# Modulation stage of a hybrid diffusion layer: plain fp32 products, a scale row and one shift addition

## The chip, the cores and the metric

The kernel runs as one program on one core of a Trainium2 chip. The metric is device time in microseconds (us) from launch to end. The kernel before took 2781.36 us (median of three runs, 2778.57 to 2790.45). Its profiled execution took 2780.29 us, of which the trace covers a span of 2778.5 us.

## The reference

One layer works on 2048 latent tokens and 256 context tokens of width 1024. What matters here is its first step:

```
c_act = silu(c);  cctx_act = silu(c_ctx)
mod_lat = c_act @ ada_w + ada_b          # 6 parts of 1024: sh1, sc1, g1, sh2, sc2, g2
mod_ctx = cctx_act @ ada_w + ada_b
h_ctx = rmsnorm(ctx, norm1_g) * (1 + csc1) + csh1
h_lat = rmsnorm(x + pos, norm1_g) * (1 + sc1) + sh1
proj = h @ w_in                          # for both streams, then three token mixers
x = x + g1 * (y @ w_out);  x = x + g2 * sq_relu_mlp(...);  out = rmsnorm(x, final_g)
```

The norm divides each token by its root mean square. The factor (1 + sc1) * norm1_g and the shift sh1 belong to the 1024 features and are the same for all latent tokens; the context has its own pair.

## The kernel before, in words

The engines are TensorE (PE; its weight loads are PEld), VectorE (DVE), ScalarE (ACT), GpSimd (POOL) and SyncE (SP), which issues nearly all DMAs. PE runs its instructions in the order in which the program writes them. The orders of the other engines come from a scheduler that goes by priorities; `high_priority` raises them. Each engine works through its own list in order, so an instruction that waits holds up all behind it.

The first stage has these steps, with the lines of the kernel before:

- Modulation (L265 to L298). The first 2048 columns of `ada_w` (shift and scale) come in 32 tiles `aw` of 128x512. Each is split for the product into a rounded part (ACT, L274) and a rest (DVE or POOL, L275), both of the type fp32r, and two products (L276, L277) add into four PSUM tiles `m`. The rows are copied (L285), transposed (L287) and added to the bias, so that `mT` (shift) and `sc1` (scale) hold one feature per partition and a column for each stream.
- Norm (`norm_in`, L240, with `rstd_of`, L212). A tile is 128 tokens, one per partition, 1024 features along it. There are 18: t0 and t1 are context, t2 to t17 latents. For a latent tile POOL adds two position parts (L237, L238). ACT squares and sums (L251) and takes a first reciprocal root (L215, L216), DVE corrects it in three small operations (L218, L221, L225) and multiplies the tile by both factors (L253).
- Modulate (`modulate`, L436). PE transposes a tile in two halves of four blocks (L444), so that features lie on partitions. DVE (L448, five blocks) and ACT (L450, three blocks) read them from PSUM with the block's scale and shift into `hy`; ACT rounds (L451) into `hTh`, and DVE or POOL takes the rest (L452) into `hTl`. In the loop the norm of tile i+2 is written ahead of the modulate of tile i; the first four tiles are normed before the loop.
- Products. Five token groups: group 0 is t0 and t1, the others four latent tiles each. Two weight blocks are loaded and split beforehand (L312, L313), and the products of a group with them (L365 to L367, three per feature block) are slipped in behind the tiles of the next group by a `Filler`. The last group's products follow the loop, and after them come the other projections and the mixers.

The token tiles `xt` have four buffers: t4's load has to wait for the transposes of t0, and so on.

Of the kernel before, what the change touches and what calls it, by code (L numbers as in the profile page):

```python
# [20 lines left out]
P = 128  # L21
# [90 lines left out]
def body(ctx: ExitStack, tc: tile.TileContext, I, out, dbg=None, stage=99):  # L112
# [16 lines left out]
    def trt():  # L129
        return ps.tile([P, 512], F32, name="tr", bufs=1)  # L130
# [44 lines left out]
    csp = const.tile([P, KC, 4], F32R, name="csp")  # L175
# [7 lines left out]
    nc.vector.tensor_copy(csp[:, :, 0:2], cact)  # L183
    nc.vector.tensor_tensor(csp[:, :, 2:4], cact, csp[:, :, 0:2].bitcast(F32), op=ALU.subtract)
# [55 lines left out]
    def norm_in(g, j):  # L240
        t0 = GRP[g][0]
        xt = nrm.tile([P, D], F32, name="xt", bufs=4)
        if g == 0:
            nc.sync.dma_start(xt, cx[j * P:(j + 1) * P, :])
        else:
            i = (t0 - CTX) // P + j
            nc.sync.dma_start(xt, x[i * P:(i + 1) * P, :])
            add_pos(nrm, posc, i, xt)
        ss = nrm.tile([P, 1], F32, name="ss", bufs=3)
        junk = nrm.tile([P, D], mybir.dt.bfloat16, name="junk", bufs=1)  # L250
        nc.scalar.activation(junk, xt, AF.Square, accum_out=ss)  # L251
        r0, r1 = rstd_of(nrm, ss, 1, D, "n1")
        nc.vector.tensor_scalar(xt, xt, r0, r1, op0=ALU.mult, op1=ALU.mult)  # L253
        return xt
# [11 lines left out]
    for k in range(KC):  # L266
        for j in range(4):
            i = 4 * k + j
            with tc.high_priority(PRI + 1500):
                aw = adp.tile([P, 512], F32, name="aw", bufs=8)  # L270
                nc.sync.dma_start(aw, ada_w[k * P:(k + 1) * P, 512 * j:512 * j + 512])
                ah = adp.tile([P, 512], F32R, name="awh", bufs=3)
                al = adp.tile([P, 512], F32R, name="awl", bufs=3)
                nc.scalar.copy(ah, aw)  # L274
                (nc.gpsimd if i % 5 in (0, 2) else nc.vector).tensor_tensor(al, aw, ah.bitcast(F32), op=ALU.subtract)  # L275
            nc.tensor.matmul(mps[j][0:4, :], csp[:, k, :], ah, start=k == 0, stop=False)  # L276
            nc.tensor.matmul(mps[j][0:2, :], csp[:, k, 0:2], al, start=False, stop=k == KC - 1)  # L277
# [3 lines left out]

    mtp = trt()
    for j in range(4):
        mrow = adp.tile([4, 512], F32, name="mrow", bufs=2)
        (nc.vector.tensor_copy if j % 2 else nc.scalar.copy)(mrow, mps[j][0:4, :])  # L285
        for i in range(4):
            nc.tensor.transpose(mtp[:, 16 * j + 4 * i:16 * j + 4 * i + 4], mrow[:, i * P:(i + 1) * P], ident[0:4, 0:4])  # L287
# [3 lines left out]
    mtv = mtp[:, 0:64].rearrange("p (j s) -> p j s", s=4)  # L291
    nc.vector.tensor_tensor(mT, mtv[:, :, 0:2],
                            pcol("ab", 0, 16).unsqueeze(2).to_broadcast([P, 16, 2]), op=ALU.add)
    nc.vector.tensor_tensor(mT, mT, mtv[:, :, 2:4], op=ALU.add)
# [141 lines left out]
    def modulate(g, j, xt):  # L436
        s = 1 if g == 0 else 0
        ts_ = slice(j * P, (j + 1) * P)
        for hf in range(2):
# [5 lines left out]
            for k in range(4):  # L445
                kk = 4 * hf + k
                if k < 2 + hf:
                    nc.vector.tensor_scalar(y[:, k, :], tp[:, k, :], sc1[:, kk, s:s + 1], mT[:, kk, s:s + 1], op0=ALU.mult, op1=ALU.add)  # L448
                else:
                    nc.scalar.activation(y[:, k, :], tp[:, k, :], AF.Identity, scale=sc1[:, kk, s:s + 1], bias=mT[:, kk, s:s + 1])  # L450
# [3 lines left out]
    for i, (g, j) in enumerate(tiles):  # L454
        if NA <= i + 2 < len(tiles):
            xts[tiles[i + 2]] = norm_in(*tiles[i + 2])
        modulate(g, j, xts.pop((g, j)))
# [1361 lines left out]
```

## Time and profile before

| | before |
|---|---|
| median of three runs | 2781.36 us |
| profiled execution | 2780.29 us |
| span of its trace | 2778.5 us |
| first stage, up to the last group's first product | 138.4 us |
| PE busy over the span | 92% |

The profile names a group of instructions by line, engine, operation and tiles. Busy time is the time in which an engine had an instruction running; idle time before an instruction is put down to what released it. The granted clock is a share of TensorE's full rate.

### The profile page before, as it was taken

How to read it: one execution, taken by the hardware profiler on the slowest of the kernel's cores; microseconds unless marked ns; L12 is line 12 of the kernel's file. 1: busy time of each engine (PE TensorE's matmuls, PEld its weight loads, DVE VectorE, ACT ScalarE, POOL GpSimd, SP SyncE). 2: the span in 40 equal slices, each digit the busy share in tenths (PEclk: the TensorE clock that was granted, in tenths of full speed). 3: DMA queues.
4: the chain of work that ended last, by engine and by line, in shares of the span. 5: the costliest groups of instructions: out<-in, count | busy, mean ns of one | idle time of the engine just before them, and what ended most of it. 6: DMA issues, size and time to landing. Idle time of an engine off the chain costs nothing. (4 is left out here: it accounts for less than half of the span.)

```text
span 2778.5 us, 36372 instructions
## 1 busy us (share of the span) xinstructions
PE 2561.5 (92%) x12239; PEld 2081.4 (75%) x12239; DVE 1754.9 (63%) x3039; ACT 1161.4 (42%) x2053; POOL 982.4 (35%) x868
## 2 busy tenths in 40 slices
PE   5798889899999888888897999989999999999997
PEld 3676667788887676777776888867887888888876
DVE  7855476146646986656665787666666356545586
ACT  6755521133335666433334444544445332222343
POOL 5734411245444443334443343343432122222221
PEclk8999989999999999989998999999999999999999
DMA  7443355565656666766663777555554677656564
GB/s 221 143 138 110 95 159 163 155 159 157 156 153 174 183 177 187 242 192 203 233 204 104 205 211 223 171 183 163 144 156 139 221 244 242 211 176 202 169 210 152
DMA packets 490215, 495.24 MB, mean 178 GB/s; under 512 B 88226, under 2 KB 371580, under 8 KB 490028
## 3 DMA queue, kind: packets, MB, share of 16 engines
q1 hardware_dynamic: 464076, 465.58, 55.7%
q10 hardware_dynamic: 20480, 15.73, 1.7%
q0 software_dynamic: 5472, 11.60, 1.5%
q8 instruction: 97, 1.59, 0.2%
q14 instruction: 90, 0.74, 0.1%
HBM read 336.89 MB, written 155.92 MB: 177 GB/s over the span
## 5 line engine op out<-in xcount | busy, mean ns | idle before, releaser
L365 PE MATMUL pp<-hTh,whi 128*128 128x512 f32 (+1 forms) x1048 | 435.6, 416 | 14.5 <-DVE evt L505 10.9
L367 PE MATMUL pp<-hTh,wlo 128*128 128x512 f32 (+1 forms) x1048 | 410.4, 392 | 1.7 <-POOL wlo L313 1.3
L366 PE MATMUL pp<-hTl,whi 128*128 128x512 f32 (+1 forms) x1048 | 408.8, 390 | 0.2 <-DVE hTl L452 0.2
L1780 PE MATMUL yps<-bh,al 128*128 128x512 f32 x832 | 326.5, 392 | 3.8 <-POOL al L1405 2.4
L1778 PE MATMUL yps<-bh,ah 128*128 128x512 f32 x832 | 325.7, 392 | 0.0
L1779 PE MATMUL yps<-bl,ah 128*128 128x512 f32 x832 | 324.2, 390 | 0.0
L1405 POOL TENSOR_TENSOR al<-ar,ah 128x1024 fp32r<-128x1024 f32 x54 | 132.6, 2455 | 481.3 <-ACT ah L1642 470.8
L365 PEld LDWEIGHTS pp<-hTh,whi 128*128 128x128 f32 x1048 | 206.0, 197 | 52.0 <-DVE evt L505 12.7
L1642 ACT CAST ah<-ar 128x1024 fp32r<-128x1024 f32 x108 | 113.5, 1051 | 306.2 <-PE yps L1779 270.4
L367 PEld LDWEIGHTS pp<-hTh,wlo 128*128 128x128 f32 x1048 | 204.7, 195 | 45.6 <-POOL wlo L313 3.5
L366 PEld LDWEIGHTS pp<-hTl,whi 128*128 128x128 f32 x1048 | 205.6, 196 | 35.5 <-issue 1.9
L1780 PEld LDWEIGHTS yps<-bh,al 128*128 128x128 f32 x832 | 156.2, 188 | 42.9 <-POOL al L1405 4.3
L1779 PEld LDWEIGHTS yps<-bl,ah 128*128 128x128 f32 x832 | 156.3, 188 | 33.4
L1778 PEld LDWEIGHTS yps<-bh,ah 128*128 128x128 f32 x832 | 156.4, 188 | 31.9
L1408 POOL TENSOR_TENSOR uz<-tz 128x512 f32<-128x512 f32 x32 | 49.8, 1556 | 345.2 <-ACT whi L1413 176.2
L1478 PE MATMUL accy<-th,whi 128*128 128x512 f32 x384 | 152.6, 397 | 2.2 <-ACT th L1642 1.2
L1480 PE MATMUL accy<-th,wlo 128*128 128x512 f32 x384 | 150.7, 392 | 2.6 <-DVE wlo L1405 2.6
L1479 PE MATMUL accy<-tl,whi 128*128 128x512 f32 x384 | 151.0, 393 | 0.0
L1405 DVE TENSOR_TENSOR wlo<-wab,whi 128x512 fp32r<-128x512 f32 x124 | 115.2, 931 | 36.3 <-ACT whi L1413 36.3
L1405 DVE TENSOR_TENSOR wlo<-ws,whi 128x512 fp32r<-128x512 f32 x93 | 78.5, 845 | 81.8 <-ACT whi L1413 81.5
L1413 ACT CAST whi<-wab 128x512 fp32r<-128x512 f32 x124 | 76.7, 619 | 120.3 <-PE accy L1479 54.8
L1264 PE MATMUL pp<-woh,yh 128*128 128x512 f32 x256 | 106.2, 415 | 9.0 <-ACT yh L1250 9.0
(407 smaller groups left out, 6040.1 us busy)
## 6 DMA issues: line engine op xcount, KB each, us to landing
uD<-uz SPq DMA_DIRECT2D x224, 256.0 KB
ar<-uD SPq DMA_DIRECT2D x108, 512.0 KB
braw<-in_mlp_w_dram SPq DMA_DIRECT2D x84, 512.0 KB
wab<-in_mlp_w_dram SPq DMA_DIRECT2D x62, 512.0 KB
maw<-in_ada_w_dram SPq DMA_DIRECT2D x64, 256.0 KB
wraw<-in_w_in_dram SPq DMA_DIRECT2D x54, 256.0 KB
rb<-rD SPq DMA_DIRECT2D x96, 128.0 KB
aw<-in_ada_w_dram SPq DMA_DIRECT2D x32, 256.0 KB
```

The costliest lines, as they stand in the source:

```text
L365: nc.tensor.matmul(acc[:, 0:n], hi, hTh[g][:, k, :], start=k == 0, stop=False)
L366: nc.tensor.matmul(acc[:, 0:n], hi, hTl[g][:, k, :], start=False, stop=False)
L367: nc.tensor.matmul(acc[:, 0:n], lo, hTh[g][:, k, :], start=False, stop=k == KC - 1)
L1264: nc.tensor.matmul(acc, yh[:, k, :], woh[:, k, ns], start=k == 0, stop=False)
L1405: eng.tensor_tensor(o, a, b, op=ALU.subtract)
L1478: nc.tensor.matmul(acc, hi[:, k, :], T2[i][0][:, k, :], start=first and k == 0, stop=False, skip_group_check=True)
L1479: nc.tensor.matmul(acc, hi[:, k, :], T2[i][1][:, k, :], start=False, stop=False, skip_group_check=True)
L1480: nc.tensor.matmul(acc, lo[:, k, :], T2[i][0][:, k, :], start=False, stop=k == 3, skip_group_check=True)
L1642: nc.scalar.copy(hi, r_)
L1778: nc.tensor.matmul(acc, ah[:, p_, :], bh, start=p_ == 0, stop=False)
L1779: nc.tensor.matmul(acc, ah[:, p_, :], bl, start=False, stop=False)
L1780: nc.tensor.matmul(acc, al[:, p_, :], bh, start=False, stop=p_ == 7)
```

## The change

- `ada_w` tiles are no longer split: one plain fp32 product of each tile with `cact` takes the place of two fp32r products, and `csp` goes.
- The latents' scale is also built as a row: the bias and norm gain come in as rows of 1024 (`arow`, `nrow`, two small loads on SP), two additions and two products on one partition give (1 + scale) * gain, and two plain fp32 products with a column of ones spread it over 128 partitions into `scB` (copied from PSUM by ACT and DVE).
- For a latent tile the norm's last multiplication is gone. The two factors are multiplied with each other (128x1), and `modulate` multiplies the tile by that and by `scB` ahead of the transposes (after L450). Out of PSUM comes one addition of the shift per half (after L458, DVE) where five DVE and three ACT operations stood. Context tiles keep the old way.

Line numbers differ between the two kernels; L456 of the kernel after is the transpose of L444, L463 and L465 are L448 and L450, L467 is L452, L322 and L323 are L312 and L313, L215, L218 and L222 the norm's small operations.

DVE's list of the kernel before, from the last context operations to the first latent ones (`tp_575` and `tp_587` are t1's transposes, `tp_618` t2's first half):

```order
L448 TENSOR_SCALAR hy<-tp_575,sc_494,mT 128x128 x2
L448 TENSOR_SCALAR hy<-tp_587,sc_494,mT 128x128 x3
L218 TENSOR_SCALAR n1v<-ss 128x1
L312 CAST whi<-evt 128x512
L452 TENSOR_TENSOR hTl_87<-hy,hTh_86 128x4x128
L313 TENSOR_TENSOR wlo<-evt,whi 128x512
L218 TENSOR_SCALAR n1v<-ss 128x1
L221 SCALAR_TENSOR_TENSOR n1t<-n1r,n1v 128x1
L225 TENSOR_SCALAR n1t<-n1t 128x1
L253 TENSOR_SCALAR xt<-xt,n1r,n1t 128x1024
```

The same stretch of DVE's list in the kernel after (`n1r` and `n1t` from here on are t2's and t3's factors, `row_297` the scale row, `pp` the spread row, `tp_404` t0's transposes):

```order
L215 TENSOR_SCALAR n1v<-ss 128x1 x2
L218 SCALAR_TENSOR_TENSOR n1t<-n1r,n1v 128x1 x2
L222 TENSOR_SCALAR n1t<-n1t 128x1 x2
L253 TENSOR_TENSOR n1r<-n1r,n1t 128x1 x2
L291 SCALAR_TENSOR_TENSOR row_297<-row_297,mrow 1x512 x2
L292 TENSOR_TENSOR row_297<-row_297,row_296 1x512 x2
L322 CAST whi<-wraw 128x512
L323 TENSOR_TENSOR wlo<-wraw,whi 128x512
L322 CAST whi<-wraw 128x512
L298 COPY scB<-pp 128x512
L322 CAST whi<-evt 128x512 x2
L323 TENSOR_TENSOR wlo<-wraw,whi 128x512
```

Before, both context tiles are modulated ahead of the factors of t2 and t3. Now the factors of t2 and t3 stand first, the row behind them, and the context tiles' L463 come only after eight weight operations and the copy L298 more (three of these weight operations lie behind the rows shown).

PE's list of the kernel before, from the last modulation product to t2's transposes (`m` are the PSUM tiles of the modulation, `tp_551` to `tp_587` the context's transposes):

```order
L277 MATMUL m_199<-awl,csp 2x512
L279 MATMUL tr<-ident,pr 128x128
L287 MATMUL tr<-ident,mrow 128x4 x16
L444 MATMUL tp_551<-ident,xt 128x128 x4
L444 MATMUL tp_563<-ident,xt 128x128 x4
L444 MATMUL tp_575<-ident,xt 128x128 x4
L444 MATMUL tp_587<-ident,xt 128x128 x4
L444 MATMUL tp_618<-ident,xt 128x128 x4
```

And the same place in the kernel after:

```order
L271 MATMUL m_196<-aw,cact 2x512
L273 MATMUL tr<-ident,pr 128x128
L294 MATMUL tr<-ident,mrow 128x2 x16
L297 MATMUL pp<-row_297,row_298 128x512 x2
L456 MATMUL tp_404<-ident,xt 128x128 x4
L456 MATMUL tp_416<-ident,xt 128x128 x4
L456 MATMUL tp_428<-ident,xt 128x128 x4
L456 MATMUL tp_440<-ident,xt 128x128 x4
```

The two products that spread the row now stand between the modulation and the context's transposes. From the end of the first stage on, the lists of all engines are the same in both kernels.

```diff
--- before.py
+++ after.py
@@ -172,7 +172,6 @@
     crt = trt()
     nc.tensor.transpose(crt[:, 0:2 * KC], cr, ident[0:2 * KC, 0:2 * KC])
     cact = const.tile([P, KC, 2], F32, name="cact")
-    csp = const.tile([P, KC, 4], F32R, name="csp")
     sgt = const.tile([P, 2 * KC], F32, name="sgt")
     nc.vector.tensor_scalar(sgt, crt[:, 0:2 * KC], -87.0, None, op0=ALU.max)
     nc.scalar.activation(sgt, sgt, AF.Exp, scale=-1.0)
@@ -180,8 +179,6 @@
     nc.vector.reciprocal(sgt, sgt)
     nc.vector.tensor_tensor(cact, crt[:, 0:2 * KC].rearrange("p (s k) -> p k s", s=2),
                             sgt.rearrange("p (s k) -> p k s", s=2), op=ALU.mult)
-    nc.vector.tensor_copy(csp[:, :, 0:2], cact)
-    nc.vector.tensor_tensor(csp[:, :, 2:4], cact, csp[:, :, 0:2].bitcast(F32), op=ALU.subtract)
     pr = sm.tile([P, P], F32, name="pr")
     nc.vector.memset(pr, 0.0)
     srcs = [
@@ -250,8 +247,11 @@
         junk = nrm.tile([P, D], mybir.dt.bfloat16, name="junk", bufs=1)
         nc.scalar.activation(junk, xt, AF.Square, accum_out=ss)
         r0, r1 = rstd_of(nrm, ss, 1, D, "n1")
-        nc.vector.tensor_scalar(xt, xt, r0, r1, op0=ALU.mult, op1=ALU.mult)
-        return xt
+        if g == 0:
+            nc.vector.tensor_scalar(xt, xt, r0, r1, op0=ALU.mult, op1=ALU.mult)
+            return xt, None
+        nc.vector.tensor_tensor(r0, r0, r1, op=ALU.mult)
+        return xt, r0
 
     tiles = [(g, j) for g in range(5) for j in range(GRP[g][1] // P)]
     xts = {}
@@ -265,33 +265,43 @@
     mps = [pm0.tile([P, 512], F32, name=f"m{i}") for i in range(4)]
     for k in range(KC):
         for j in range(4):
-            i = 4 * k + j
             with tc.high_priority(PRI + 1500):
                 aw = adp.tile([P, 512], F32, name="aw", bufs=8)
                 nc.sync.dma_start(aw, ada_w[k * P:(k + 1) * P, 512 * j:512 * j + 512])
-                ah = adp.tile([P, 512], F32R, name="awh", bufs=3)
-                al = adp.tile([P, 512], F32R, name="awl", bufs=3)
-                nc.scalar.copy(ah, aw)
-                (nc.gpsimd if i % 5 in (0, 2) else nc.vector).tensor_tensor(al, aw, ah.bitcast(F32), op=ALU.subtract)
-            nc.tensor.matmul(mps[j][0:4, :], csp[:, k, :], ah, start=k == 0, stop=False)
-            nc.tensor.matmul(mps[j][0:2, :], csp[:, k, 0:2], al, start=False, stop=k == KC - 1)
+            nc.tensor.matmul(mps[j][0:2, :], cact[:, k, :], aw, start=k == 0, stop=k == KC - 1)
     prt = trt()
     nc.tensor.transpose(prt[:, 0:P], pr, ident)
     nc.vector.tensor_copy(prm, prt[:, 0:P])
 
+
+    nrow, arow, ones1 = [adp.tile([1, w_], F32, name=f"row{w_}{i}") for i, w_ in enumerate((D, D, P))]
+    with tc.high_priority(PRI + 1000):
+        nc.sync.dma_start(nrow, I["norm1_g"])
+        nc.sync.dma_start(arow, ada_b[D:2 * D].rearrange("(o n) -> o n", o=1))
+    hot = ExitStack()
+    hot.enter_context(tc.high_priority(PRI + 1500))
+    nc.vector.memset(ones1, 1.0)
     mtp = trt()
-    for j in range(4):
-        mrow = adp.tile([4, 512], F32, name="mrow", bufs=2)
-        (nc.vector.tensor_copy if j % 2 else nc.scalar.copy)(mrow, mps[j][0:4, :])
+    scB = sm.tile([P, D], F32, name="scB")
+    for j in (2, 3, 0, 1):
+        mrow = adp.tile([2, 512], F32, name="mrow", bufs=4)
+        (nc.vector.tensor_copy if j % 2 else nc.scalar.copy)(mrow, mps[j][0:2, :])
+        if j >= 2:
+            js = slice(512 * j - D, 512 * j - D + 512)
+            nc.vector.scalar_tensor_tensor(arow[:, js], arow[:, js], 1.0, mrow[0:1, :], op0=ALU.add, op1=ALU.add)
+            nc.vector.tensor_tensor(arow[:, js], arow[:, js], nrow[:, js], op=ALU.mult)
         for i in range(4):
-            nc.tensor.transpose(mtp[:, 16 * j + 4 * i:16 * j + 4 * i + 4], mrow[:, i * P:(i + 1) * P], ident[0:4, 0:4])
+            nc.tensor.transpose(mtp[:, 8 * j + 2 * i:8 * j + 2 * i + 2], mrow[:, i * P:(i + 1) * P], ident[0:2, 0:2])
+    for hf in range(2):
+        sb = pp()
+        nc.tensor.matmul(sb, ones1, arow[:, 512 * hf:512 * hf + 512])
+        (nc.vector.tensor_copy if hf else nc.scalar.copy)(scB[:, 512 * hf:512 * hf + 512], sb)
+    hot.close()
     adst.close()
     alloc_h(spool(hlat, "hp4", "left"), 4)
     mT = const.tile([P, 16, 2], F32, name="mT")
-    mtv = mtp[:, 0:64].rearrange("p (j s) -> p j s", s=4)
-    nc.vector.tensor_tensor(mT, mtv[:, :, 0:2],
-                            pcol("ab", 0, 16).unsqueeze(2).to_broadcast([P, 16, 2]), op=ALU.add)
-    nc.vector.tensor_tensor(mT, mT, mtv[:, :, 2:4], op=ALU.add)
+    mtv = mtp[:, 0:32].rearrange("p (j s) -> p j s", s=2)
+    nc.vector.tensor_tensor(mT, mtv, pcol("ab", 0, 16).unsqueeze(2).to_broadcast([P, 16, 2]), op=ALU.add)
 
     sc1 = const.tile([P, KC, 2], F32, name="sc1")
     nc.vector.scalar_tensor_tensor(sc1, mT[:, 8:16, :], 1.0, pcol("n1", 0, KC).unsqueeze(2).to_broadcast([P, KC, 2]),
@@ -433,28 +443,33 @@
     wxa = [load_half(w_in, [(C_XA, 0, P)], P, hf, w0 if hf else None, True) for hf in range(2)]
     pt0 = psum(p0, "pt0")
 
-    def modulate(g, j, xt):
+    def modulate(g, j, xt, rs):
         s = 1 if g == 0 else 0
         ts_ = slice(j * P, (j + 1) * P)
+        if g:
+            nc.vector.scalar_tensor_tensor(xt, xt, rs, scB, op0=ALU.mult, op1=ALU.mult)
         for hf in range(2):
             tp = pt0.tile([P, 4, P], F32, name="tp0", bufs=4)
             y = nrm.tile([P, 4, P], F32, name="hy", bufs=3)
             ks = slice(4 * hf, 4 * hf + 4)
             for k in range(4):
                 nc.tensor.transpose(tp[:, k, :], xt[:, (4 * hf + k) * P:(4 * hf + k + 1) * P], ident)
-            for k in range(4):
-                kk = 4 * hf + k
-                if k < 2 + hf:
-                    nc.vector.tensor_scalar(y[:, k, :], tp[:, k, :], sc1[:, kk, s:s + 1], mT[:, kk, s:s + 1], op0=ALU.mult, op1=ALU.add)
-                else:
-                    nc.scalar.activation(y[:, k, :], tp[:, k, :], AF.Identity, scale=sc1[:, kk, s:s + 1], bias=mT[:, kk, s:s + 1])
+            if g:
+                nc.vector.tensor_tensor(y, tp, mT[:, ks, 0:1].to_broadcast([P, 4, P]), op=ALU.add)
+            else:
+                for k in range(4):
+                    kk = 4 * hf + k
+                    if k < 2 + hf:
+                        nc.vector.tensor_scalar(y[:, k, :], tp[:, k, :], sc1[:, kk, s:s + 1], mT[:, kk, s:s + 1], op0=ALU.mult, op1=ALU.add)
+                    else:
+                        nc.scalar.activation(y[:, k, :], tp[:, k, :], AF.Identity, scale=sc1[:, kk, s:s + 1], bias=mT[:, kk, s:s + 1])
             nc.scalar.copy(hTh[g][:, ks, ts_], y)
             (nc.gpsimd if hf else nc.vector).tensor_tensor(hTl[g][:, ks, ts_], y, hTh[g][:, ks, ts_].bitcast(F32), op=ALU.subtract)
 
     for i, (g, j) in enumerate(tiles):
         if NA <= i + 2 < len(tiles):
             xts[tiles[i + 2]] = norm_in(*tiles[i + 2])
-        modulate(g, j, xts.pop((g, j)))
+        modulate(g, j, *xts.pop((g, j)))
         if g and j == 1:
             fil.add(f"first{g - 1}", first(g - 1), GRP[g - 1][1] / 50)
         fil.run(2.7)
```

## Rows read from the trace of the kernel before

**Rows 1.** The page: busy time, share of the span and instructions.
```profile
PE 2561.5 (92%) x12239; PEld 2081.4 (75%) x12239; DVE 1754.9 (63%) x3039; ACT 1161.4 (42%) x2053; POOL 982.4 (35%) x868
```

**Rows 2.** Stretches from:to: length, busy (instructions) per engine, clock, DMA share, GB/s.
```profile
30.00:56.00 26.00, 13.70 (x68) 10.06 (x68) 20.20 (x44) 12.47 (x30) 12.79 (x11) 0.61 0.81 205
56.00:139.00 83.00, 59.57 (x297) 49.37 (x295) 73.56 (x158) 63.93 (x153) 61.55 (x48) 0.88 0.45 136
139.00:165.00 26.00, 25.89 (x123) 21.64 (x124) 12.66 (x24) 7.43 (x14) 7.43 (x13) 1.00 0.51 144
```

**Rows 3.** Timeline, modulation: start us, length us, engine, line, operation, [idle before].
```profile
1.92 24.37 SPq L271 DMA_DIRECT2D aw<-in_ada_w_dram  x32
...
11.78 0.63 PE L277 MATMUL m<-awl,csp 128*2 128x512 f32 x1
12.20 0.63 PE L276 MATMUL m<-awh,csp 128*4 128x512 f32 x1
...
16.36 0.39 PE L277 MATMUL m<-awl,csp 128*2 128x512 f32 x1
16.58 0.40 PE L276 MATMUL m<-awh,csp 128*4 128x512 f32 x1
...
32.34 0.40 PE L277 MATMUL m<-awl,csp 128*2 128x512 f32 x1
```

**Rows 4.** Timeline, plain fp32 products later in the program (L574).
```profile
181.57 3.60 PE L574 MATMUL qk<-xc,gw 128*128 128x512 f32 x8
```

**Rows 5.** Timeline, from the context tiles to the first latent tile.
```profile
38.13 1.94 PE L444 MATMUL tp<-ident,xt 128*128 128x128 f32 x8 [2.76 <-DVE n1v L218]
...
46.56 1.06 ACT L251 ACTIVATE junk<-xt 128x1024 bf16<-128x1024 f32 x1 [0.76 <-POOL xt L237]
...
56.66 1.99 DVE L448 TENSOR_SCALAR hy<-tp,sc,mT 128x128 f32<-128x128 f32 x6
```

**Rows 6.** DVE's groups, 56 to 139 us: busy, mean ns | idle before.
```profile
L448 DVE TENSOR_SCALAR hy<-tp,sc,mT 128x128 f32<-128x128 f32 x80 | 29.0, 402 | 2.5 <-PE tp L444 1.7
L452 DVE TENSOR_TENSOR hTl<-hy,hTh 128x512 fp32r<-128x512 f32 x16 | 18.6, 1165 | 1.4 <-ACT hTh L451 1.4
L253 DVE TENSOR_SCALAR xt<-xt,n1r,n1t 128x1024 f32<-128x1024 f32 x14 | 16.8, 1201 | 0.3
L221 DVE SCALAR_TENSOR_TENSOR n1t<-n1r,n1v 128x1 f32<-128x1 f32 x14 | 7.0, 499 | 1.5 <-ACT n1r L216 1.5
```

**Rows 7.** DVE's groups of the whole program, by form.
```profile
L1405 DVE TENSOR_TENSOR al<-ar,ah 128x1024 fp32r<-128x1024 f32 x54 | 65.9, 1220 | 21.9 <-ACT ah L1642 21.7
...
L684 DVE SCALAR_TENSOR_TENSOR macc<-maw,cact,macc 128x512 f32<-128x512 f32 x56 | 42.1, 753 | 21.3 <-DMA maw<-in_ada_w_dram 20.5
L1408 DVE TENSOR_TENSOR yu<-yps,yu 128x512 f32<-128x512 f32 x56 | 38.5, 687 | 84.9 <-PE yps L1780 84.8
```

**Rows 8.** Timeline, POOL's and DVE's operations side by side and apart.
```profile
98.95 1.29 POOL L238 TENSOR_TENSOR xt<-xt,posc 128x512 f32<-128x512 f32 x1
...
98.99 1.26 DVE L221 SCALAR_TENSOR_TENSOR n1t<-n1r,n1v 128x1 f32<-128x1 f32 x1 [0.28 <-ACT n1r L216]
...
102.15 0.68 DVE L452 TENSOR_TENSOR hTl<-hy,hTh 128x512 fp32r<-128x512 f32 x1
...
103.78 0.20 DVE L221 SCALAR_TENSOR_TENSOR n1t<-n1r,n1v 128x1 f32<-128x1 f32 x1
...
104.89 0.80 DVE L253 TENSOR_SCALAR xt<-xt,n1r,n1t 128x1024 f32<-128x1024 f32 x1
```

**Rows 9.** ACT's groups of scale, shift and rounding, 56 to 139 us.
```profile
L450 ACT ACTIVATE hy<-tp,mT,sc 128x128 f32<-128x128 f32 x48 | 20.9, 451 | 16.0 <-DVE hy L448 12.4 <-DVE n1v L218 1.8 <-DVE n1t L221 1.1
L451 ACT CAST hTh<-hy 128x512 fp32r<-128x512 f32 x32 | 19.0, 617 | 0.2
```

**Rows 10.** Timeline, the last latent tile and the last group's first product.
```profile
133.25 1.37 DVE L448 TENSOR_SCALAR hy<-tp,sc,mT 128x128 f32<-128x128 f32 x4
...
138.38 0.50 PE L365 MATMUL pp<-hTh,whi 128*128 128x512 f32 x1 [1.52 <-ACT hTh L451]
```

## The prediction

> **What bounds the kernel now.** I read the page first: TensorE is busy 92% of the span [rows 1], so only a stretch in which it waits can move the end. The stretches show where. From 30 to 56 us PE is busy 13.7 of 26 us at a granted clock of 0.61, from 56 to 139 us 59.6 of 83, and from 139 us on it has no gap to speak of (25.9 of 26) [rows 2]. Everything that the change touches lies before 139 us. Since the lists of all engines behind it are the same, I take the rest of the program as moved rigidly: the time changes by as much as the last group's first product (L365) moves from 138.38 us [rows 10].
>
> In 56 to 139 us DVE is the busiest engine, 73.6 of 83 us, with ACT at 63.9 and POOL at 61.6 [rows 2]. Its groups say what fills it: the shift and scale out of PSUM (L448), the rest of the split (L452), the norm's product (L253), the small L221 [rows 6]. The first latent L448 starts at 56.66 us and t17's at 133.25 [rows 5, 10], 15 tiles apart, so a tile takes 5.11 us.
>
> **The products of the modulation.** Before, two fp32r products per tile start 0.42 us apart while the matmuls take 0.63 us, and 0.22 us apart with 0.39 us each later, a pace near 1.2 and 2.4 GHz for 512 columns; the last starts at 32.34 us [rows 3]. Plain fp32 exists in this trace: one call of `gates` issues four products (L574), which stand as eight records in 3.60 us [rows 4]. Less 0.17 us for the last one's end, by which 0.39 exceeds 0.22 above, that is 0.43 us per record and 0.86 us, two records, per product. 32 of them are 27.5 us at the full rate; starting at 5 us, with the slow pace (1.73 us each) for the first 5 to 9 us, they end between 35 and 37 us, 3 to 5 us later than now. The splits on ACT, DVE and POOL go, but nothing else is ready then: SP is busy with `aw` until 26.3 us [rows 3], and the tokens are loaded after it. So freeing three engines there is worth nothing. The later end costs nothing by itself either, since the next step waits for something later; only the loads behind `aw` can slip, as a buffer of `aw` is now free when its product is done: 0 to 2 us.
>
> **The start (term A).** This is the large one. In the new lists PE cannot transpose the context before the two products with the row, and DVE builds the row only after the factors of t2 and t3. Those need POOL's position additions and ACT's squares. Before, ACT's square of t3 starts at 46.56 us, released by POOL [rows 5]; I take 1.2 us off because POOL no longer has a split of the context in between. Square, root and three dependent small operations twice bring DVE to 48.4 us. The row is 4 operations of about 0.69 us (nearest: 0.687 and 0.753 for 512 columns [rows 7]); I count them at 512 columns although they lie on one partition. The first product can start after the third, 50.4 us. PE has been idle by then, and the rows show what it does after idling: eight transposes take 1.94 us [rows 5], the slow level. So the two products take 1.73 us each, to 53.9, and the context's 16 transposes 3.9 us, to 57.8, where the first eight started at 38.13 before. DVE meanwhile waits for the spread row at 54 us (L298), does the weight splits that stand behind it until 57.6, then ten L448 (0.36 each) and two L452 (0.68), then the two new multiplications of t2 and t3, and waits some 2 us in between because ACT's list has the square of t4 ahead, whose load waits for t0's transposes. The first latent addition out of PSUM comes near 68.2 us, 11.5 behind the 56.66 of before. DVE's operations overlap a little where I laid them end to end; I take A = +10. Lower end +5 (full clock, no wait for t4); upper end +15 (loads slip 2 us, DVE is held up by POOL).
>
> **The pace (term B).** Per latent tile on DVE: five L448 (29.0/16 = 1.81 us) become two additions of 128x512 from PSUM; the nearest row is L1408 at 0.687 [rows 7], 1.37 in all: -0.44. L253, mean 1.20 where an undisturbed one is 0.80 [rows 6, 8], becomes a two-tensor operation of 128x1024: 1.22 by L1405, 1.5 by twice L684 [rows 7]; I take 1.28 undisturbed, and the same 0.39 of hold-up on top: +0.47. The new 128x1 product costs 0.20 as an undisturbed L221 [rows 8], 0.50 as a mean one [rows 6]: I take 0.20, because it follows a sibling directly. Together +0.23 per tile, 15 tiles: B = +3.5. ACT loses three operations of 0.45 us per tile [rows 9], but ACT was not the bound: 12.4 of its 16.0 us before L450 were spent waiting for DVE. DVE's own waits for ACT are 1.5 + 1.4 us in all [rows 6], the most that can come back there.
>
> The hold-up is in the rows: L221 takes 1.26 us at 98.99, while POOL's 1.29 us addition from 98.95 runs, and 0.20 at 103.78 with no POOL addition beside it [rows 8]. The Trainium skill ("SBUF — State Buffer", "Who interferes with whom") says that a DVE instruction with two SBUF inputs contends with a GpSimd instruction that reads SBUF, and that the later one blocks fully. The trace agrees with the blocking here. By that rule the change adds to the contending side (the 128x1024 product and one more small one per tile); what it would make of the time is the second rival.
>
> **The tail (term C).** From t17's first L448 to the last group's first product it is 138.38 - 133.25 = 5.1 us [rows 10]. With one addition (0.69) and ACT's rounding (L451, 0.62 [rows 9]) ahead of it, and half a microsecond of waits, that shrinks to about 1.7: C = -3.4; if it doesn't shrink, 0.
>
> **Sum.** +10 + 3.5 - 3.4 = +10 on the profiled execution's 2780.3 us, which stands 1.1 below the median: 2790 us.
>
> **Rivals.**
> First, DVE's hold-ups vanish. If POOL falls out of step with DVE, the mean operations drop to the undisturbed ones: L452 by 1.165 - 0.68, L221 by 0.30, the new product by 0.39, which makes the pace -0.44 + 0.08 + 0.20 - 0.48 - 0.30 = -0.94 per tile, B = -14, and the time 2780.3 + 10 - 14 - 3.4 = 2773. From a gain of 0.45 per tile on, the kernel is not slower. For it: ACT is lighter and DVE no longer shares `hy` with it. Against: POOL keeps its three operations per tile, busy 61.6 of 83 us. 18%.
>
> Second, DVE and POOL exclude each other and set the pace. Three POOL operations of 1.29 [rows 8] and DVE's two-input operations (0.80 + 0.68 + 0.20) are 5.55 us per tile, above the 5.11 measured, so it isn't strictly so yet; after, DVE's share is 1.28 + 0.68 + 0.20 + 0.20, 0.68 more. B = +10, the time 2797. It speaks against the change, and the mean of L452, 1.165 against 0.68, speaks for it. 20%.
>
> Third, the start is mostly hidden: DVE does the same work in another order, and only PE's two products and the row are new, 3.5 + 2.8 us, of which half is covered by weight splits. A = +3, the time 2783. Against it stand the waits of PE's list, which can't be passed. 15%.
>
> Fourth, the fp32 products stay at the slow level, 32 x 1.73 = 55 us, ending at 60 us; the `aw` buffers then hold back the tokens' loads by about 17 us: 2807. Against it: before, PE reached 2.4 GHz by 16.4 us with more gaps than it will have. 4%.
>
> **How the numbers follow.** The forecast, 2790, has 43%, its own range 2783 to 2797. With the rivals 80% lie between 2774 and 2802. Half a per cent, about what a measurement of this kernel can tell from no change, is 13.9 us of 2781.4: slower means over 2795.3, faster under 2767.5. Slower: a fifth of the forecast (9%), most of the second rival (12%), the fourth (4%): 25%. Faster: a third of the first rival, 7%. Within: 68%.
>
> **What would show it.** After: 32 products, two records each, 0.43 us per record, the last ending at 35 to 37 us; the context's first transposes near 54 us with the idle time before them put down to the row (L292 or L297's operands); the first latent L458 near 67 us; 5.3 us from tile to tile; L450 at 1.3 to 1.7 us and L458 at 0.69; the last group's first product near 148 us, and from there the same trace as before, 10 us later. I am wrong in A if the transposes start before 50 us, in B if a tile takes under 4.9 or over 5.7 us, and in the rigid shift if the gap between the two kernels at 150 us isn't that at the end.

## The result, and the profile after

The changed kernel takes **2815.6 us** (median; 2811.5 to 2817.0), the kernel before 2780.3 in the same series: ratio **1.0112, 95% interval 1.0087 to 1.0137**. It is slower, by 35 us where 10 were forecast and 2802 was the upper end of the wider range (80%). The profiled execution has a span of 2814.7 us, 36.2 more than before's 2778.5.

First the start, which answers to [rows 3, 5]: the timeline of the changed kernel (start us, length us, engine, line, operation, [idle before <- releaser]). L271 are the plain fp32 products, L292 builds the row, L297 spreads it, L456 are the transposes, L450 multiplies the latents by the row, L458 is their shift out of PSUM.
```profile
5.28 29.45 PE L271 MATMUL m<-aw,cact 128*2 128x512 f32 x64 [1.66 <-DMA aw<-in_ada_w_dram]
...
49.68 1.27 DVE L292 TENSOR_TENSOR row<-row,row 1x512 f32<-1x512 f32 x2
50.41 3.77 PE L297 MATMUL pp<-row,row 1*128 1x512 f32 x4 [12.90 <-DVE row L292]
...
54.12 3.67 PE L456 MATMUL tp<-ident,xt 128*128 128x128 f32 x16
...
63.82 3.59 DVE L450 SCALAR_TENSOR_TENSOR xt<-xt,n1r,scB 128x1024 f32<-128x1024 f32 x2
...
69.01 0.68 DVE L458 TENSOR_TENSOR hy<-tp,mT 128x512 f32<-128x512 f32 x1
```
The 32 products are 64 records and end at 34.7 us. PE idles 12.9 us for the row, the context is transposed at 54.12 instead of 38.13, and the first latent sum comes at 69.01 instead of 56.66: 12.35 us late.

Next the stretches that answer to [rows 2], and DVE's groups of the stretch in which the latent tiles run, 69 to 159 us, which answer to [rows 6] (busy us, mean ns of one | idle before).
```profile
30.00:69.00 39.00, 16.88 (x64) 9.46 (x62) 23.54 (x49) 13.87 (x33) 14.94 (x12) 0.62 0.62 162
69.00:159.00 90.00, 60.66 (x300) 50.88 (x299) 77.48 (x121) 45.83 (x101) 67.00 (x46) 0.82 0.35 117
```
```profile
L450 DVE SCALAR_TENSOR_TENSOR xt<-xt,n1r,scB 128x1024 f32<-128x1024 f32 x14 | 28.7, 2057 | 0.5
L458 DVE TENSOR_TENSOR hy<-tp,mT 128x512 f32<-128x512 f32 x31 | 20.8, 681 | 1.3 <-POOL hTl L467 1.2
L467 DVE TENSOR_TENSOR hTl<-hy,hTh 128x512 fp32r<-128x512 f32 x16 | 15.0, 938 | 3.5 <-ACT hTh L466 3.3
L253 DVE TENSOR_TENSOR n1r<-n1r,n1t 128x1 f32<-128x1 f32 x14 | 7.4, 527 | 0.0
L218 DVE SCALAR_TENSOR_TENSOR n1t<-n1r,n1v 128x1 f32<-128x1 f32 x14 | 7.2, 518 | 1.7 <-ACT n1r L213 1.6
```
ACT fell to 45.8 of 90 us, but DVE (77.5) and POOL (67.0) have no less to do. L450 takes 2.06 us on average, L253 0.53. Their own rows, beside POOL's and alone (L234, L235 add the positions):
```profile
89.29 1.74 POOL L467 TENSOR_TENSOR hTl<-hy,hTh 128x512 fp32r<-128x512 f32 x1
...
89.87 2.24 DVE L450 SCALAR_TENSOR_TENSOR xt<-xt,n1r,scB 128x1024 f32<-128x1024 f32 x1
90.96 2.27 POOL L235 TENSOR_TENSOR xt<-xt,posc 128x512 f32<-128x512 f32 x1
92.03 1.23 DVE L253 TENSOR_TENSOR n1r<-n1r,n1t 128x1 f32<-128x1 f32 x1
...
111.54 0.15 DVE L253 TENSOR_TENSOR n1r<-n1r,n1t 128x1 f32<-128x1 f32 x1
...
111.78 1.28 DVE L450 SCALAR_TENSOR_TENSOR xt<-xt,n1r,scB 128x1024 f32<-128x1024 f32 x1
```
Read the first four together: L450 ends 1.08 us after POOL's L467 (91.03 to 92.11), POOL's L235 1.12 us after L450, L253 right after L235. The two engines take turns; a product of 128x1 waits 1.1 us for its turn. Alone, L450 takes 1.28 us and L253 0.15.

Last the late program, in which the instruction lists of both kernels are the same. `gates` is the first product of a mixer, behind the first stage; the MLP up and MLP down products end the program. Pools of tiles are stacked from both ends, the left and the right side, of each partition's memory. In MLP down, the last stage, the weights (`bh`, `bl`, the moving tiles of 128x512) come in 14 chunks, the even ones in a left-side pool, the odd ones in a right-side pool; what they are multiplied with (`ah`, `al`, the stationary tiles of 128x128) lies right. Of before: the first product of `gates`; two rows of the MLP up stage, two even-chunk and two odd-chunk rows of the last stage, each pair 90 products apart; and the last product.
```profile
170.09 1.97 PE L574 MATMUL qk<-xc,gw 128*128 128x256 f32 x8 [3.01 <-DMA xc<-xcD]
...
1954.61 0.39 PE L1478 MATMUL accy<-th,whi 128*128 128x512 f32 x1
...
1975.21 0.39 PE L1478 MATMUL accy<-th,whi 128*128 128x512 f32 x1
...
2406.99 0.40 PE L1778 MATMUL yps<-bh,ah 128*128 128x512 f32 x1
...
2427.61 0.40 PE L1778 MATMUL yps<-bh,ah 128*128 128x512 f32 x1
...
2450.97 0.40 PE L1778 MATMUL yps<-bh,ah 128*128 128x512 f32 x1
...
2471.42 0.39 PE L1778 MATMUL yps<-bh,ah 128*128 128x512 f32 x1
...
2764.00 0.39 PE L1780 MATMUL yps<-bh,al 128*128 128x512 f32 x1
```
Of after, the first shift of the last latent tile and then the same places:
```profile
157.01 0.68 DVE L458 TENSOR_TENSOR hy<-tp,mT 128x512 f32<-128x512 f32 x1
...
192.41 2.94 PE L589 MATMUL qk<-xc,gw 128*128 128x256 f32 x8 [3.44 <-issue]
...
1979.81 0.39 PE L1493 MATMUL accz<-th,whi 128*128 128x512 f32 x1
...
2000.81 0.39 PE L1493 MATMUL accy<-th,whi 128*128 128x512 f32 x1
...
2441.06 0.39 PE L1793 MATMUL yps<-bh,ah 128*128 128x512 f32 x1
...
2462.06 0.40 PE L1793 MATMUL yps<-bh,ah 128*128 128x512 f32 x1
...
2485.86 0.39 PE L1793 MATMUL yps<-bh,ah 128*128 128x512 f32 x1
...
2506.28 0.39 PE L1793 MATMUL yps<-bh,ah 128*128 128x512 f32 x1
...
2800.28 0.39 PE L1795 MATMUL yps<-bh,al 128*128 128x512 f32 x1
```
At `gates` the changed kernel is 22.3 us late, at the last product 36.3. Without a wait between them, products of the even chunks start 21.00/90 = 233.3 ns apart where it was 20.62/90 = 229.1; those of MLP up, whose moving tiles all lie left, 21.00/90 = 233.3 where it was 20.60/90 = 228.9; the odd chunks have 226.9 and 227.2. PE's busy time on the page [rows 1] went from 2561.5 to 2595.8 us: a good part of the loss isn't waiting, it is the same products taking longer. What the change did to them is their place: `csp`, 128 bytes per partition of the pool `const`, is gone, and all tiles on the left side of the SBUF behind it lie 128 bytes lower. In these stages the tiles of the right side stay.

### The profile page after: what moved, and what is told of

Its sections match the earlier page's. It is cut to its first block, busy times and chain, and to the rows that moved or that the text cites. A ratio compares the mean times of both kernels' runs of the same rounds, so it can differ in the third digit from the quotient of the medians.

```text
span 2814.7 us, 36133 instructions
## 1 busy us (share of the span) xinstructions
PE 2595.8 (92%) x12243; PEld 2087.2 (74%) x12243; DVE 1741.5 (62%) x2991; ACT 1127.0 (40%) x1974; POOL 974.3 (35%) x855
## 5 line engine op out<-in xcount | busy, mean ns | idle before, releaser
L1794 PEld LDWEIGHTS yps<-bl,ah 128*128 128x128 f32 x832 | 156.2, 188 | 35.2
L323 POOL TENSOR_TENSOR wlo<-wraw,whi 128x512 fp32r<-128x512 f32 x54 | 73.9, 1369 | 119.1 <-ACT whi L322 107.3
```

The source lines that it names most:

```text
L1794: nc.tensor.matmul(acc, ah[:, p_, :], bl, start=False, stop=False)
```

## The experiments

How late some places are against the kernel before, in us, from one trace of each (0 is before's own time). No trace holds addresses: the places modulo 512 bytes that the texts give are those that the build of each kernel gave its tiles.

| place (time before) | after | e1 | e2 | e5 |
|---|---|---|---|---|
| `gates` (170.09) | 22.3 | 22.2 | 0.3 | -0.7 |
| first MLP up product (1479.90) | 22.8 | 13.3 | 1.1 | -2.5 |
| first MLP down product (2144.39) | 30.5 | 18.7 | 8.5 | -8.1 |
| last product (2764.00) | 36.3 | 20.0 | 14.2 | -7.7 |

**e1, the changed kernel at the old addresses.**
```diff
+    pad = const.tile([P, 32], F32, name="pad")
+    nc.vector.memset(pad, 0.0)
```


> The changed kernel, with a tile of 32 fp32 values per partition that nobody reads in the const pool, where csp was. The tiles of the later stages then stand at the addresses that they have in the kernel before; the first stage is the changed one. Placement theory: the 14 us that the changed kernel loses after its first stage come from csp's 128 bytes, which moved every tile of the left-side pools; they come back, 2800 to 2804 us, and the last stage's products start every 229.0 and 227.0 ns in turn as before, not 233.3 and 227.0. Rival, phase theory: the later loss comes from the shift in time of the first stage, by which weight loads meet other work; the time stays at 2813 to 2818 us and 233.3 ns stays. What either leaves is the first stage's loss, some 22 us.


Measured: 2801.0 us, ratio 1.0084 (1.0066 to 1.0101); even chunks 229.0 ns again. An unread tile gives back 14.6 us. The trace doesn't give it all back where e2, below, loses it: of the 16.3 us at the last product, 9.4 come between `gates` and MLP up, a stretch of 1300.9 us here, 1309.8 before and up to 1315.7 in the traces of this case. And in MLP up, from 1894 us to the end of the stage, products are 21.00/90 = 233.3 ns apart at the addresses of before, with the granted clock at 1.00, where the first half has 229:
```profile
1974.35 0.40 PE L1495 MATMUL pp<-th,whi 128*128 128x512 f32 x1
...
1995.35 0.40 PE L1495 MATMUL accz<-th,whi 128*128 128x512 f32 x1
```
So the place alone doesn't fix the pace here.

**e2, the kernel before at the new addresses.**
```diff
-    csp = const.tile([P, KC, 4], F32R, name="csp")
+    csp = sm.tile([P, KC, 4], F32R, name="csp")
```


> The kernel before, with csp allocated in the pool sm instead of const: the instructions and their order are the same, only the left-side pools behind const stand 128 bytes lower, as in the changed kernel. Placement theory: first stage as before, then the changed kernel's loss of its later stages without its first stage: 2790 to 2797 us, 233.3 ns in the even chunks of the last stage. Phase theory: nothing is moved in time, so 2778 to 2784 us and 229.0 ns.


Measured: 2793.4 us, ratio 1.0056 (1.0039 to 1.0072), 233.3 ns in the even chunks. With every engine's list the same, PE is busy 14.8 us longer than in [rows 1]:
```profile
PE 2576.3 (92%) x12239; PEld 2074.7 (74%) x12239; DVE 1755.2 (63%) x3039; ACT 1161.4 (42%) x2053; POOL 986.4 (35%) x868
```
MLP up has 233.3 ns as well. The phase theory falls as the cause of the later loss: it is there without any shift in time, in the same two stages. The medians of e1 and e2 add up (21.4 + 13.8 = 35.2 us, the whole loss), by e1's trace partly by chance.

**e3, another place.** The kernel before, plus an unread `const` tile of `[P, 56]`.


> The kernel before with an unread tile of 224 bytes per partition in const: the left-side pools stand 224 bytes higher (the even chunks' weights at 0 modulo 512 where they were at 288). Placement theory: the pace of products that read left-side tiles moves again and that of the odd chunks (right-side tiles) stays at 227.0 ns; where to isn't known from two values, 222 to 235 ns, so 2760 to 2800 us in all. Phase theory: 2778 to 2784 us, 229.0 ns.


Measured: 2792.8 us, ratio 1.0057 (1.0037 to 1.0076), 233.3 and 227 ns. The place counts, but a multiple of 512 isn't a good one.

**e4, the fp32 products alone** (diff: `csp`, `awh`, `awl` and the splits removed, one fp32 product per tile; nothing else).


> The kernel before with one part of the change: the modulation as plain fp32 products (no split into two halves, csp replaced by an unread tile of its size so that nothing behind it moves); scale and shift are applied as before, without the row. My steps say that these products end with the weights' loads and cost nothing: 2776 to 2784 us. Rival: they are the start's loss, 2788 to 2794 us, with the first latent tile's sum out of PSUM 10 us or more later than before.


Measured: 2780.8 us, ratio 1.0006 (0.9991 to 1.0021). Within that interval (-2.5 to +5.8 us) this part of the change costs nothing and brings nothing.

**e5, left side as the right.** As e3, with `[P, 48]`.


> The kernel before with an unread tile of 192 bytes per partition in const: the weights of the even chunks of the last stage then stand at 480 modulo 512 bytes, where those of the odd chunks stand anyway (288 was 229.0 ns, 160 and 0 were 233.3 ns, 480 on the right side is 227.0 ns). If the place modulo 512 is what counts, even chunks go at 227.0 ns, and the whole at 2768 to 2777 us. If the left and the right side differ for another reason, 229 or 233 ns and 2779 to 2795 us.


Measured: 2773.2 us, ratio 0.9981 (0.9972 to 0.9990): a little faster than before. Two rows of an even chunk, 90 products apart:
```profile
2400.94 0.39 PE L1780 MATMUL yps<-bh,ah 128*128 128x512 f32 x1
...
2421.34 0.39 PE L1780 MATMUL yps<-bh,ah 128*128 128x512 f32 x1
```
20.40/90 = 226.7 ns, as in the odd chunks. The last stage is no shorter for it in this trace (620.0 us from its first product to its last, 619.6 before), as PE waits longer between products; the gain lies in MLP up.

**e6, the row behind the context.**
```diff
-    for hf in range(2):
-        sb = pp()
-        nc.tensor.matmul(sb, ones1, arow[...])
-        (nc.vector.tensor_copy if hf else nc.scalar.copy)(scB[...], sb)
...
     for i, (g, j) in enumerate(tiles):
...
+        if i == 2:
+            (the same four lines)
```


> The changed kernel with the addresses of before in the later stages, and with the two products that spread the scale row, and their copies out of PSUM, issued behind the context tiles' transposes instead of ahead of them (the row is built in place in scB, and its ones come from the unread tile). By my term A the start is lost because PE holds the context's transposes back for the row: then they run near 38 to 42 us, the first latent sum out of PSUM comes near 56 to 60 us instead of 69, and the time is 2789 to 2794 us, against 2801 with the row in front. Rival: DVE's work and the position additions set the start, the transposes move and the first latent sum stays near 66 to 69 us: 2798 to 2802 us.


Measured: 2790.0 us, ratio 1.0043 (1.0031 to 1.0055); `gates` 15.8 us late instead of 22.2. Transposes, DVE's copy of the row, the first sum:
```profile
39.80 1.34 PE L453 MATMUL tp<-ident,xt 128*128 128x128 f32 x8 [1.97 <-DVE n1v L217]
```
```profile
53.99 0.41 DVE L319 CAST whi<-evt 128x512 fp32r<-128x512 f32 x1
...
59.06 1.49 DVE L319 CAST whi<-evt 128x512 fp32r<-128x512 f32 x1
...
61.67 0.68 DVE L473 COPY scB<-pp 128x512 f32<-128x512 f32 x1
...
64.99 0.69 DVE L455 TENSOR_TENSOR hy<-tp,mT 128x512 f32<-128x512 f32 x1
```
The time is what my term A said, the first sum lies between both theories: the context no longer waits, but DVE does the splits of the first weights (L319, L320) ahead of the copy, and some of them are held up (L319 at 1.49 us, beside a POOL addition, where another takes 0.41). L319 reads only one operand from the SBUF.

**e7 and e8, no position additions.** Left out in both: `add_pos(nrm, posc, i, xt)`.


> The changed kernel with the addresses of before in the later stages, without the addition of the position rows to the latents in the first stage (two POOL additions of 128x512 and two DMAs per tile are left out). Hold-up theory: DVE's product with the scale row takes 2.2 us instead of 1.28 only where a POOL addition runs beside it, and this sets the pace; without the additions its mean falls to 1.3 to 1.5 us, the small 128x1 products to 0.2 to 0.5, the pace per latent tile from 5.87 to 4.5 to 5.0 us, and the time to 2783 to 2793 us. Rival, order and waits: the product's time doesn't change or the pace stays at 5.6 us or more though it does: 2797 to 2802 us.

> The kernel before without the same position additions, as the other half of that test. Hold-up theory: DVE's time before is less exposed to POOL (reads from PSUM, 128x128 pieces); the pace of 5.11 us per latent tile falls less than in the changed kernel, to 4.7 to 5.1 us, 2771 to 2780 us. Rival: POOL's additions themselves bound both kernels' pace, which then fall by the same 0.7 us per tile or more, 2766 to 2771 us.


Measured: 2771.6 us, ratio 0.9970 (0.9954 to 0.9986), and 2757.8 us, 0.9926 (0.9912 to 0.9941). Both fell by more than either theory said, as the start came earlier too (first sum 59.40 and 52.89 us; 68.59 in e1, 56.66 before). The pace per latent tile, from the first sum of t2 to that of t17, is free of that: it falls from 5.89 (e1) to 4.56 in the changed kernel, by 1.33, and from 5.17 to 4.22 in the one before, by 0.95. So most of what the additions cost both kernels pay, as e8's rival had it; the changed one pays 0.38 us per tile more, and of the 0.72 us between the two paces 0.33 are left. In e7 the first sums of t2 and t17 and the scale product's mean are
```profile
59.40 0.68 DVE L459 TENSOR_TENSOR hy<-tp,mT 128x512 f32<-128x512 f32 x1
...
127.76 1.29 DVE L459 TENSOR_TENSOR hy<-tp,mT 128x512 f32<-128x512 f32 x2
```
```profile
L451 DVE SCALAR_TENSOR_TENSOR xt<-xt,n1r,scB 128x1024 f32<-128x1024 f32 x14 | 20.8, 1490 | 0.0
```
1.49 us where it was 2.06. The changed kernel's pace was more exposed to POOL, but that is about half of the difference in pace; 6.5 of the 12 us at the first sum stay as well.

**e9, both sides moved.** e5, and
```diff
+    rpad = ctx.enter_context(tc.tile_pool(name="rpad", bufs=1, side="right")).tile([P, 48], F32, name="rpad")
+    nc.vector.memset(rpad, 0.0)
```


> The kernel before with the left-side pools 192 bytes higher (480 modulo 512, as in e5) and all right-side pools 192 bytes lower (480 becomes 288). In the last stage the moving tile lies left in even chunks and right in odd ones; the stationary tile lies right in both. If the moving tile's own place modulo 512 sets the pace: even chunks 227.0 ns, odd chunks 229.0 ns. If the distance between moving and stationary tile sets it: odd chunks stay at 227.0 ns (both were moved) and even chunks leave 227.0 ns. If nothing on the right side counts: 227.0 in both. The whole: 2770 to 2785 us.


Measured: 2793.6 us, ratio 1.0054 (1.0035 to 1.0072). Even chunk, then odd chunk:
```profile
2426.86 0.39 PE L1782 MATMUL yps<-bh,ah 128*128 128x512 f32 x1
...
2447.86 0.39 PE L1782 MATMUL yps<-bh,ah 128*128 128x512 f32 x1
...
2471.66 0.39 PE L1782 MATMUL yps<-bh,ah 128*128 128x512 f32 x1
...
2492.08 0.39 PE L1782 MATMUL yps<-bh,ah 128*128 128x512 f32 x1
```
21.00/90 = 233.3 and 20.42/90 = 226.9 ns. The even chunks' moving tiles stand where they were in e5 (226.7 ns), and are slow; the odd ones' stand at 288, where before had 229 ns, and are fast. So the place of the moving tile alone doesn't decide; its distance from the stationary tile fits both. The whole is longer than the 2770 to 2785 us expected.

**e10, an early row.** e6, with the loads of `nrow` and `arow` ahead of the modulation's weights and both copies on ScalarE.


> As e6 (row products behind the context's transposes, addresses of before), and besides the row's two inputs are loaded ahead of the modulation's weights, so that the row is built right behind the products (near 36 to 39 us instead of 50 to 54), and ScalarE makes both copies of the spread row. If the late row is what keeps the first latent sum late (64.99 in e6), it comes at 57 to 61 us and the time is 2783 to 2788 us. Rival: VectorE's splits of the first weights and the held-up position additions set the first latent tile; it stays at 62 us or later, and the time at 2787 to 2792 us.


Measured: 2789.6 us, ratio 1.0045 (1.0029 to 1.0060); the row is built at 35.4 to 39.9 us, the first sum still comes at 62.24, 2.75 ahead of e6. The rival was right: most of what is left of the start isn't the row but DVE's other work, splits of weights that last until 59.7 us.

**e11, the row kept in PSUM.** e10, and
```diff
-            nc.vector.scalar_tensor_tensor(xt, xt, rs, scB, op0=ALU.mult, op1=ALU.mult)
+            for hf in range(2):
+                h_ = slice(512 * hf, 512 * hf + 512)
+                nc.vector.scalar_tensor_tensor(xt[:, h_], xt[:, h_], rs, scP[hf], op0=ALU.mult, op1=ALU.mult)
...
-            tp = pt0.tile([P, 4, P], F32, name="tp0", bufs=4)
+            tp = pt0.tile([P, 4, P], F32, name="tp0", bufs=2)
```


> As e10, but the spread scale row stays in PSUM (two banks, taken from the buffers of the latents' transposes, two instead of four), so that the latents' scale product reads one operand from PSUM, in two halves of 128x512. If VectorE is held up beside POOL only where both its operands lie in SBUF, as the trace has it (the shift's addition out of PSUM never takes over 0.69 us), each half takes 0.65 to 0.75 us throughout, the pace per latent tile falls from 5.7 to 4.9 to 5.3 us, and the time to 2774 to 2782 us. Rival: it is held up the same way (halves of 1.1 to 1.2 us), or the two buffers fewer set the pace: 5.6 us or more, 2784 to 2792 us.


Measured: 2780.9 us, ratio 1.0004 (0.9990 to 1.0017). The groups of e10 (DVE, POOL), then of e11:
```profile
L447 DVE SCALAR_TENSOR_TENSOR xt<-xt,n1r,scB 128x1024 f32<-128x1024 f32 x15 | 27.8, 1854 | 0.5
```
```profile
L236 POOL TENSOR_TENSOR xt<-xt,prow 128x512 f32<-128x512 f32 x13 | 24.0, 1846 | 0.1
```
```profile
L450 DVE SCALAR_TENSOR_TENSOR xt<-xt,n1r,scP 128x512 f32<-128x512 f32 x30 | 21.8, 739 | 0.5
```
```profile
L236 POOL TENSOR_TENSOR xt<-xt,prow 128x512 f32<-128x512 f32 x13 | 16.6, 1281 | 0.0
```
Two halves of 0.74 us instead of 1.85, and POOL's addition 1.28 instead of 1.85: with one operand in PSUM neither of these two waits for the other. The Trainium skill ("SBUF — State Buffer", "Who interferes with whom") says that a DVE instruction with at most one SBUF input, outside its two-port modes, doesn't contend with GpSimd; this pair of runs agrees. The pace falls from 5.55 to 5.28 us, the upper end of what was expected; the 128x1 operations are held up as before (0.58 to 0.61 us in the mean in both runs). The first sum comes at 58.85, and of the 22 us at `gates` 3.1 are left; the total can't be told from before's.

**e12 and e15, two more distances.** e3 with `[P, 24]`; and e2 plus a `const` tile of `[P, 16]`.


> The kernel before with 96 unread bytes per partition in const: the left-side pools at 384 modulo 512. One more point of the pace against the place: known are 227.0 ns at 480, 229.0 at 288, 233.3 at 160 and at 0. If the pace falls steadily from 160 towards 480, even chunks go at 227.5 to 228.5 ns, 2774 to 2780 us; if only the last 64 bytes below a multiple of 512 are good, 229 to 233 ns, 2779 to 2793 us.

> The kernel before with csp in the pool sm and 64 unread bytes in const: left-side pools at 224 modulo 512, that is 256 from the right-side ones. Known by distance modulo 512: 0 is 227.0 ns, 320 is 229.0, 32 and 192 are 233.3, 416 is 234.3. If distances of 0 and 256 are alike, even chunks go at 227 ns and the time is 2770 to 2777 us; otherwise, between their neighbours 192 and 320, at 229 to 233 ns and 2779 to 2795 us.


Measured: e12 2800.5 us, ratio 1.0071 (1.0050 to 1.0093), 234.3 ns, a miss of my guess; e15 2776.4 us, ratio 0.9985 (0.9969 to 1.0000), 226.7 ns. The even chunks by distance, moving less stationary tile modulo 512 bytes:

| distance | 0 | 32 | 192 | 256 | 320 | 416 |
|---|---|---|---|---|---|---|
| ns per product | 226.7 (e5) | 233.3 (e3) | 233.3 (after, e2, e9) | 226.7 (e15) | 229.1 (before, e1) | 234.3 (e12) |

Distance 192 stands for two pairs of places (160 and 480 in after and e2, 480 and 288 in e9), distance 0 too (480 and 480, and 288 and 288 in e9's odd chunks).

**e13 and e14, both kernels at the best placement.** Left-side tiles as in e5, and in both, ahead of the pool `op`:
```diff
+        spool(wost, "wpad", "left").tile([P, 80], F32, name="wpad")
```


> The changed kernel as in e11 (row early, spread behind the context's transposes, kept in PSUM), with the left-side pools at 480 modulo 512 as in e5, and 320 unread bytes between the output projection's weights and its other tiles, so that these, too, stand at distance 0 modulo 512 from what they are multiplied with. From e11 (2780.9) less what e5 gained on before (5.7 us) less 768 products by 2.9 ns (2.2 us): 2771 to 2775 us, with 227.0 ns in all the late stages. Rival: the gains of placement are hidden by other waits in the changed kernel: 2776 to 2782 us.

> The kernel before with the placement of e13 alone: left-side pools at 480 modulo 512 as in e5, and the 320 unread bytes in the output projection. Distance theory: the output projection's products, 229.7 to 229.9 ns apart in all runs though their tiles moved by up to 224 bytes together, fall to 227.0 ns, since for the first time the distance between the two operands is changed (from 320 to 0 modulo 512); the whole goes from e5's 2773.2 to 2769 to 2773 us. Rival, own place or something else on the left side: they stay at 229.5 ns or more, 2772 to 2775 us.


Measured: the changed kernel (as e11) 2773.5 us, ratio 0.9980 (0.9965 to 0.9995); the one before 2771.5 us, 0.9971 (0.9957 to 0.9984). Both beat before, and don't differ from each other. The output projection's products went from a median of 229 to 227 ns, but their mean only from 229.7 to 229.1, since about a quarter of them takes 231 to 236: the distance theory's 227.0 came true for most products of this stage, not for all.

## Why the prediction was wrong

**The rigid move failed**, and cost the most. I wrote that the program behind 138.38 us moves as a whole; its lists do, its addresses didn't. Between `gates` and the last product another 14.0 us are lost, the size of e2's loss (13.8), which has none of the change but the 128 bytes: products of MLP up and of MLP down's even chunks start 233.3 ns apart, where it was 229. The diff showed it (`csp` leaves `const`), and I priced it at nothing.

**Term B was mis-sized.** The latent tiles take (157.01 - 69.01)/15 = 5.87 us. Before's pace I had read wrongly: of the four operations from 133.25 us [rows 10] three are t16's second half, as DVE's list shows, and t17's first starts at 134.22, so that before takes 5.17 us, not 5.11. The change costs 0.70 per tile, not 0.23: B is 10.4, not 3.5. L458 (0.68), and L450 and L253 undisturbed (1.28, 0.15), were right. The hold-up was not: I carried over L253's old 0.39 us to L450, which is held up by 0.78; I priced the 128x1 product at 0.20, and it takes 0.53; the old L452's shrank by 0.23. 0.23 + 0.39 + 0.33 - 0.23 = 0.72, close to the 0.70. This is the second rival's mechanism (B = +10), to which I gave 20%. Runs show it in part: without POOL's additions 0.39 of the 0.72 us between the paces go, and the 0.33 left are near the 0.24 that the new work costs undisturbed (-0.44 + 0.48 + 0.20) (e7, e8); with the row in PSUM L450 isn't held up at all, and the pace falls by 0.27 (e10, e11).

**Term A was right in size**, 12.35 for 10: the transposes at 54.12 against "near 54", the first sum at 69.01 against 68.2. Its cause was half right. The first sum comes at 68.59 in e1, at 64.99 with the context freed (e6, 6.4 us earlier at `gates`), at 62.24 with the row early (e10), at 58.85 with the row in PSUM (e11), and at 56.66 before. Without POOL's additions the two kernels are 6.5 us apart there (e7, e8). What the last 2.2 us are is open.

**Term C failed.** From t17's first shift to `gates` it is 35.40 us, and 35.87 before: C was -0.5, not -3.4. I took it that ACT's rounding sets when PE goes on, but the wait for it was only the 1.52 us of [rows 10], and after the change PE has products to do all the while (26.00 of 26 us):
```profile
160.00:186.00 26.00, 26.00 (x125) 21.50 (x124) 10.72 (x23) 7.40 (x14) 7.35 (x12) 1.00 0.53 151
```
12.35 + 10.4 - 0.5 = 22.3, the lateness at `gates`.

**The fp32 products** ended at 34.7 us, just ahead of 35 to 37, and cost nothing (e4).

Of the 26 us between forecast and result, 14 are placement, 7 the pace, 2 A and 3 C. Of the three signs named as proof against me, two came: a tile over 5.7 us, and a gap at the end that isn't the one at 150 us.

## What to carry to other kernels

Removing or adding a tile in a pool that lives through the program moves everything stacked behind it: before calling the rest of a program unchanged, compare the addresses as well as the instructions, and separate the two with an unread tile of the same size. Where VectorE and GpSimd both work on SBUF operands in the same stretch, don't carry over the hold-up that an operation has now. Add up the undisturbed times of both engines' operations that can hold each other up, before and after: here 5.55 and 6.23 us per tile. They are no forecast of the pace (5.17 and 5.87 were measured), but their difference, 0.68, came near the measured 0.70. Leaving one operand in PSUM took L450 out of the contest; one SBUF operand is no sure sign of it, as the cast L319 shows (1.49 and 0.41 us).

## What the hardware showed that I had not expected

The same 128x128 by 128x512 products start 226.7 to 234.3 ns apart at full granted clock, depending on the distance of moving and stationary tile in the SBUF; 0 and 256 bytes modulo 512 were the best of six distances. Distance isn't all of it: at 320, where nearly all products have 229 ns, half of the MLP up stage of e1 has 233.3. Over the program this is 27 us between e5 and e12 (2773.2 and 2800.5), of which e12's part isn't all explained by the pace, since its products are only 1 ns slower than e2's and its time 7 us longer. Why distance counts, what puts e1's products at the slower pace, and why about a quarter of the output projection's products stays at 231 to 236 ns at distance 0, is open.
